# The machine estimate by which the scheduler fills the queues is exchanged

## The chip, the cores and the metric

The kernel runs on one core of a Trainium2 chip. The metric is the device time of one execution in microseconds. Five engines work beside each other, each from a queue of its own that it takes in order: TensorE (PE; its weight loads are listed as PEld), VectorE (DVE), ScalarE (ACT), GpSimd (POOL) and SyncE (SP). All DMAs of this kernel are issued from SP's queue (SPq).

## The reference

One layer over 512 positions of width 1024: two branches of the normed input, a causal depthwise convolution and a recurrent scan, are gated, merged and projected, and a feed-forward block with a squared relu follows. What is computed, shortened:

```python
def hybrid_layer(x, c, ...):
    mod = jax.nn.silu(c) @ w_ada + b_ada
    shift1, scale1, gate1, shift2, scale2, gate2 = jnp.split(mod, 6, axis=-1)
    h = modulate(rms_norm(x, g_norm1), shift1, scale1)
    u = h @ w_in
    u_conv, u_rwkv, u_gate = jnp.split(u, [2 * CONV_DIM, 2 * CONV_DIM + RWKV_COLS], axis=-1)
    y_conv = conformer_conv(u_conv, ...)       # 31 taps, layer norm, silu, @ w_pw
    y_rwkv = rwkv7_mix(u_rwkv, ...)            # the scan below, group norm, gate, @ w_o
    g_conv, g_rwkv = jnp.split(jax.nn.sigmoid(u_gate), N_BRANCH, axis=-1)
    merged = g_conv * y_conv + g_rwkv * y_rwkv
    x = x + gate1[:, None, :] * (merged @ w_out)
    h2 = modulate(rms_norm(x, g_norm2), shift2, scale2)
    ff = jnp.square(jax.nn.relu(h2 @ w_ff1)) @ w_ff2
    return x + gate2[:, None, :] * ff

def step(S, inp):                              # rwkv7_scan, once per position and head
    r_t, w_t, k_t, v_t, a_t, b_t = inp
    Sa = jnp.einsum('bhij,bhj->bhi', S, a_t)
    S = S * w_t[:, :, None, :] + Sa[..., None] * b_t[:, :, None, :] + v_t[..., None] * k_t[:, :, None, :]
    y = jnp.einsum('bhij,bhj->bhi', S, r_t)
    return S, y
```

## The kernel before

Activations lie with features on the 128 partitions and the 512 positions along the free axis. Every large product is a *dense block*: `wload` (L211) has SP load a 1024 x 128 piece of weights into `raw` (two buffers), ScalarE casts it to `wH` (L215) and GpSimd forms the rest `wL` (L216); `wmul` (L219) then issues 24 matmuls of 512 columns into one of three PSUM buffers `mm`, eight times the three of L223, L224 and L225. The span has 142 such loads.

The scan is done in four groups `g` of four heads, in eight chunks of 64 positions. For each group the program traces, in this order:

- `group_solve` (L704 to L736): a triangular solve on VectorE, 31 steps of two small operations (L721, L723) between transposes (L714, L729, L731).
- `window`: dense blocks whose products go elsewhere. "c" is a convolution block (two dense blocks, L516 and L520, then 31 taps on VectorE in `weighted_sum`, L145), "g" a gate block. `WINDOWS` says which stand ahead of the chain and which behind it.
- `group_solve2` (L738 to L756): 128 small matmuls (L747, L753).
- `group_chain` (L758 to L807): for each chunk, on TensorE L767 and L769; ScalarE copies the result to `F` (L772); TensorE L776; ScalarE and VectorE copy it to `UV` (L778, L779); TensorE L784; VectorE forms `sp` and the new state `S` (L791, L792, in the first chunk L788). Each of these needs the one before, and the next chunk needs `S`. The outputs `Y` (L799, L801) hang on it.
- `group_k` and `group_prep` of the next group: its k, r and v blocks, each followed by `shifted` (ScalarE L263, VectorE L264), the decays, BK, AR, transposes (L653, L675) and the products pG (L663); then `group_post` of this one.

After the fourth group come the norm of the convolution, the products with w_pw, w_o and w_out, and the feed-forward blocks.

The order on each queue is made in three ways. Up to L477 (about the first 70 us) `tc.manual_schedule()` keeps the written order. Everything behind it is ordered by the scheduler of the TileContext: as it closes, it plays the program through an estimate of the machine and, whenever an engine can take something, appends to that engine's queue the ready instruction with the best priority. The priority is the place in the program, shifted by `forward(...)` with the numbers of `FORWARD` (one per section and group). Third, `tc.issue_after`, `after_dense` and `amid` pin single pieces behind a given matmul of their own engine. An engine then takes its queue strictly as it stands: what is queued behind an instruction that waits, waits too.

```python
FORWARD = {
    "k": (10, 10, 10, 10), "solve": (127, 153, 48, -153), "window": (0, 7, -47, -43), "chain": (-98, 348, 51, 37),
    "post": (64, 3, 0, 359), "between": (49, 49, 49, 49), "norm": (300,), "silu": (-100,), "amid": (500,),
}
```

The estimate is used for the order alone. Which semaphores an instruction waits for follows from the data and from the buffers, and holds whatever the estimate thought. The context is opened in `kernel`:

## Time and profile before

| what | value |
|---|---|
| median of three runs | 1150.29 us (1146.22 to 1151.23) |
| the profiled execution, its time | 1150.57 us |
| its span, first to last instruction | 1148.8 us |
| TensorE busy | 1066.7 us (93%) |
| VectorE busy | 765.2 us (67%) |
| ScalarE busy | 494.8 us (43%) |
| GpSimd busy | 429.5 us (37%) |
| mean granted TensorE clock | 0.969 |

A busy time is the sum of an engine's records in the profiled execution; a share is of the span. The granted clock is a share of full speed; TensorE has two levels, 2.4 GHz (1.00) and 1.2 GHz (0.50), and a mean between them says how long it stood at either. Times inside the trace are counted from the start of the span.

### The profile page before, as it was taken

The numbers are of one execution on the slowest core, as the hardware profiler recorded it, in microseconds if no ns is written. First come the engines' busy times: TensorE is split into PE (matmuls) and PEld (weight loads), VectorE is DVE, ScalarE is ACT, GpSimd is POOL, SyncE is SP. The second block draws the span as 40 slices with busy tenths as digits, with TensorE's granted clock in tenths as the row PEclk, the third lists the DMA queues.
The fourth block names the chain that finished last, engine by engine and source line by source line (L and its number), as shares of the span: only waits on it lengthen the run. The fifth ranks groups of instructions, "written<-read, shape, count | busy, mean of one in ns | idle before, by whom it ended". The sixth has DMA issues, their size and how long they took to land.

```text
span 1148.8 us, 16008 instructions
## 1 busy us (share of the span) xinstructions
PE 1066.7 (93%) x6290; PEld 818.6 (71%) x6290; DVE 765.2 (67%) x1145; ACT 494.8 (43%) x805; POOL 429.5 (37%) x237
## 2 busy tenths in 40 slices
PE   6898999998799989999979999998999999999997
PEld 5675776666566767667656777886888888888886
DVE  5878787789877898688845649788613612522545
ACT  5555534646155473365566412334413322422331
POOL 4744242243222334125431234453444444444441
PEclk9999799998899999999978999999999999999998
DMA  9622142112321125112636779952333333333332
GB/s 321 217 71 69 47 138 75 51 52 73 99 91 51 42 69 175 48 47 65 202 106 195 232 243 335 284 158 67 92 95 107 93 92 94 107 93 92 98 101 76
DMA packets 188922, 136.73 MB, mean 119 GB/s; under 512 B 5424, under 2 KB 162480, under 8 KB 188848
## 3 DMA queue, kind: packets, MB, share of 16 engines
q1 hardware_dynamic: 188848, 135.73, 38.4%
q8 instruction: 49, 0.80, 0.3%
q14 instruction: 25, 0.20, 0.1%
HBM read 121.55 MB, written 14.16 MB: 118 GB/s over the span
## 4 chain that ended last, share of the span: by engine, by line
PE 65%; DVE 19%; ACT 6%; DMA 5%; issue 3%; POOL 2%; SPq 0%; DVEq 0%; ACTq 0%; POOLq 0%
PE mm L223 16%; PE mm L224 16%; PE mm L225 16%; DVE acc L145 4%; PE pG L663 2%; ACT wH L215 1%; PE Y L801 1%; DMA adaw<-in_w_ada_dram 1%; PE Y L799 1%; PE ch L767 1%; PE ch L776 1%; DVE t2k L251 1%; PE ch L784 1%; DVE t2k L1022 1%; POOL wL L216 1%
## 5 line engine op out<-in xcount | busy, mean ns | idle before, releaser
L216 POOL TENSOR_TENSOR wL<-raw,wH 128x1024 fp32r<-128x1024 f32 x142 | 341.7, 2406 | 592.9 <-ACT wH L215 503.6
L223 PE MATMUL mm<-b,wH 128*128 128x512 f32 x720 | 292.0, 406 | 4.1 <-ACT cv L516 2.9
L225 PE MATMUL mm<-b,wL 128*128 128x512 f32 x720 | 291.0, 404 | 3.7 <-POOL wL L216 2.9
L224 PE MATMUL mm<-b,wH 128*128 128x512 f32 x720 | 291.2, 404 | 2.2 <-DVE b L1032 2.1
L215 ACT CAST wH<-raw 128x1024 fp32r<-128x1024 f32 x142 | 149.1, 1050 | 290.7 <-PE mm L224 238.9
L145 DVE SCALAR_TENSOR_TENSOR acc<-z,vt,acc 128x512 f32<-128x512 f32 x232 | 173.1, 746 | 1.8
L223 PEld LDWEIGHTS mm<-b,wH 128*128 128x128 f32 x720 | 136.9, 190 | 36.4 <-issue 3.5
L225 PEld LDWEIGHTS mm<-b,wL 128*128 128x128 f32 x720 | 137.0, 190 | 36.0 <-POOL wL L216 3.7
L224 PEld LDWEIGHTS mm<-b,wH 128*128 128x128 f32 x720 | 137.0, 190 | 33.5 <-DVE b L1032 3.5
L224 PE MATMUL mm<-g,wH 128*128 128x512 f32 x328 | 128.2, 391 | 1.2 <-DVE g L1024 0.9
L223 PE MATMUL mm<-g,wH 128*128 128x512 f32 x328 | 128.4, 391 | 0.0
L225 PE MATMUL mm<-g,wL 128*128 128x512 f32 x328 | 127.8, 390 | 0.0
L1022 DVE TENSOR_TENSOR t2k<-t2k 128x512 f32<-128x512 f32 x32 | 73.1, 2288 | 57.7 <-ACT t2k L1019 57.4
L1066 DVE SCALAR_TENSOR_TENSOR x<-mm,cols,x 128x512 f32<-128x512 f32 x31 | 23.3, 751 | 114.3 <-PE mm L225 114.3
L224 PEld LDWEIGHTS mm<-g,wH 128*128 128x128 f32 x328 | 61.6, 188 | 15.4 <-DVE g L1024 2.2
L223 PEld LDWEIGHTS mm<-g,wH 128*128 128x128 f32 x328 | 61.6, 188 | 14.0 <-ACT g L1023 1.2
L225 PEld LDWEIGHTS mm<-g,wL 128*128 128x128 f32 x328 | 61.6, 188 | 12.7 <-issue 0.2
L1023 ACT CAST g<-t2k 128x512 fp32r<-128x512 f32 x32 | 19.8, 621 | 72.7 <-DVE t2k L1022 72.7
L663 PEld LDWEIGHTS pG<-AR,BK 64*128 64x128 f32 x256 | 27.2, 204 | 14.2 <-DVE G L666 4.9
L663 PE MATMUL pG<-AR,BK 64*128 64x128 f32 x256 | 32.3, 306 | 5.1 <-DVE G L666 2.0
L1024 DVE TENSOR_TENSOR g<-t2k,g 128x512 fp32r<-128x512 f32 x32 | 23.4, 736 | 19.9 <-ACT g L1023 19.9
L723 DVE TENSOR_TENSOR Y<-tm,Y 128x126 f32<-128x126 f32 (+22 forms) x124 | 31.8, 257 | 3.4
(292 smaller groups left out, 1538.8 us busy)
## 6 DMA issues: line engine op xcount, KB each, us to landing
raw<-in_w_ff_dram SPq DMA_DIRECT2D x64, 512.0 KB, 4.1
raw<-in_w_in_dram SPq DMA_DIRECT2D x54, 512.0 KB, 3.7
adaw<-in_w_ada_dram SPq DMA_DIRECT2D x10, 1024.0 KB, 7.0
t2k<-gate SPq DMA_DIRECT2D x24, 256.0 KB, 3.8
adac<-in_w_ada_dram SPq DMA_DIRECT2D x24, 256.0 KB, 3.4
wa<-in_w_ada_dram SPq DMA_DIRECT2D x11, 512.0 KB, 5.3
gate<-cv SPq DMA_DIRECT2D x16, 256.0 KB, 2.2
raw<-in_w_pw_dram SPq DMA_DIRECT2D x8, 512.0 KB, 4.2
```

The lines of the kernel that those rows point to most:

```text
L145: dve.scalar_tensor_tensor(dst if i == n - 1 else so_far, row, col, so_far, ALU.mult, ALU.add)
L215: act.copy(wH, raw)
L216: last_low[0] = pool.tensor_tensor(wL, raw, wH, ALU.subtract)
L223: steps.append(pe.matmul(acc, wH[:, kc, :], aH(kc), start=kc == 0, stop=False))
L224: steps.append(pe.matmul(acc, wH[:, kc, :], aL(kc), start=False, stop=False))
L225: steps.append(pe.matmul(acc, wL[:, kc, :], aH(kc), start=False, stop=kc == KC - 1))
L663: pe.matmul(pgs[e][:, i, :], BK[64 * e:64 * e + 64, c, C * e:C * e + 2 * C], G.AR[64 * e:64 * e + 64, b, c, :], start=True, stop=True)
L723: dve.tensor_tensor(X[:, s + 1:32, 0:w], tv, X[:, s + 1:32, 0:w], ALU.add)
L1022: dve.tensor_tensor(t, t, t, ALU.mult)
L1023: act.copy(rH(f), t)
L1024: dve.tensor_tensor(rL(f), t, rH(f), ALU.subtract)
L1066: dve.scalar_tensor_tensor(x1(j), acc, ada[:, 40 + j:41 + j], x1(j), ALU.mult, ALU.add)
```

## The change

One argument is added where the TileContext is opened: the scheduler plays the program through its timeline simulation, another estimate of the same machine, and fills the queues by the times that this gives. The program that is traced is the same, with its priorities, pins, buffers and sizes.

```diff
-    with tile.TileContext(nc) as tc:
+    with tile.TileContext(nc, schedule_with_timeline_sim=True) as tc:
         tile_block(tc, *args)
```

## Rows read from the trace of the kernel before

**Rows 1.** The page's part 1, TensorE: busy us, share of the span, instructions.
```profile
PE 1066.7 (93%) x6290; PEld 818.6 (71%) x6290; DVE 765.2 (67%) x1145; ACT 494.8 (43%) x805; POOL 429.5 (37%) x237
```

**Rows 2.** Busy time by stretch: us, busy (x instructions) per engine, clock, DMA share, GB/s.
```profile
0.00:70.00 70.00, 55.59 (x273) 43.15 (x274) 50.56 (x58) 36.38 (x59) 42.58 (x38) 0.95 0.70 221
70.00:170.00 100.00, 92.38 (x430) 71.56 (x429) 80.08 (x145) 54.68 (x88) 37.70 (x28) 0.93 0.30 88
170.00:225.00 55.00, 53.96 (x555) 35.77 (x554) 42.45 (x67) 31.44 (x63) 11.49 (x9) 1.00 0.22 68
225.00:320.00 95.00, 78.52 (x397) 59.21 (x393) 83.69 (x163) 38.34 (x65) 32.67 (x20) 0.91 0.26 79
320.00:375.00 55.00, 52.23 (x542) 34.42 (x542) 43.35 (x68) 30.22 (x62) 11.22 (x8) 1.00 0.20 61
375.00:453.00 78.00, 71.90 (x385) 55.07 (x385) 69.02 (x132) 37.39 (x64) 29.05 (x16) 1.00 0.30 91
453.00:506.00 53.00, 53.00 (x547) 34.93 (x546) 40.40 (x67) 29.96 (x61) 12.07 (x7) 1.00 0.20 62
506.00:595.00 89.00, 77.95 (x445) 55.81 (x445) 67.81 (x136) 51.13 (x83) 39.48 (x24) 0.95 0.37 118
595.00:650.00 55.00, 49.47 (x523) 33.75 (x523) 32.27 (x57) 31.21 (x65) 9.48 (x4) 0.86 0.60 192
650.00:800.00 150.00, 142.52 (x663) 115.15 (x663) 112.72 (x137) 49.46 (x65) 60.29 (x25) 1.00 0.71 224
800.00:1120.00 320.00, 318.88 (x1409) 262.27 (x1408) 127.26 (x100) 99.87 (x128) 138.73 (x58) 1.00 0.33 95
1120.00:1149.00 29.00, 20.33 (x142) 17.48 (x140) 15.55 (x26) 4.67 (x9) 4.77 (x2) 0.84 0.22 75
```

**Rows 3.** Order of time in the first chain: start us, us, engine, line, operation, tiles.
```profile
183.56 0.26 ACT L772 COPY F<-ch 128x128 f32<-128x128 f32 x1
...
184.63 0.45 PE L776 MATMUL ch<-F,G 64*64 64x64 f32 x8
...
185.42 0.28 DVE L779 COPY UV<-ch 64x128 f32<-64x128 f32 x1 [1.05 <-ACT UV L778]
...
186.82 0.45 PE L784 MATMUL ch<-UV,bkT 128*64 128x64 f32 x8
...
188.19 0.29 DVE L792 TENSOR_TENSOR S<-sp,PC 128x128 f32<-128x128 f32 x1
...
189.13 0.34 PE L767 MATMUL ch<-S,AR 64*64 64x64 f32 x4
```

**Rows 4.** Who waited for whom, TensorE, whole span: us, times, longest.
```profile
PE pv L675 <- DVE t2k L264: 8.1, 1, 8.1
...
PE mm L225 <- POOL wL L216: 2.9, 2, 1.7
```

**Rows 5.** The same view, TensorE, 595 to 650.
```profile
PE sW L747 <- DVE s L729: 6.4, 1, 6.4
```

**Rows 6.** Order of time, 279 to 298: the last dense matmul, and the shift.
```profile
279.39 0.39 PE L225 MATMUL mm<-b,wL 128*128 128x512 f32 x1
...
297.20 0.74 DVE L264 SCALAR_TENSOR_TENSOR t2k<-mm,vt,t2k 128x511 f32<-128x511 f32 x1
```

**Rows 7.** Groups of instructions, VectorE: busy us, mean ns, idle before.
```profile
L792 DVE TENSOR_TENSOR S<-sp,PC 128x128 f32<-128x128 f32 x24 | 15.0, 624 | 0.1
```

**Rows 8.** Order of time at 208, GpSimd and VectorE.
```profile
208.29 2.38 POOL L216 TENSOR_TENSOR wL<-raw,wH 128x1024 fp32r<-128x1024 f32 x1 [10.71 <-ACT wH L215]
...
208.85 1.98 DVE L792 TENSOR_TENSOR S<-sp,PC 128x128 f32<-128x128 f32 x1
```

**Rows 9.** Who waited for whom, SP's queue, whole span.
```profile
SPq L213 <- POOL wL L216: 696.1, 130, 23.3
```

**Rows 10.** Order of time, TensorE, at 604 in the last chain.
```profile
604.13 0.69 PE L776 MATMUL ch<-F,G 64*64 64x64 f32 x8 [1.88 <-ACT G L734]
...
605.58 0.70 PE L784 MATMUL ch<-UV,bkT 128*64 128x64 f32 x8
```

## The prediction

> **What bounds the kernel now.** I read the page's busy shares first: TensorE works in 1066.7 us of the 1148.8 us span [rows 1]. A change that removes no instruction can therefore win only from the 82 us in which TensorE stands idle, and from the time it spends at the lower of its two clock levels. The second view is the busy time in twelve stretches, cut where the stages of the kernel change [rows 2]. Here the reader is to see three kinds of stretch. The first 70 us (idle 14.4) are written out by hand in manual_schedule and the estimate cannot move them. From 800 on the program is a plain row of dense blocks, each with 24 matmuls that wait for nothing but their weights: idle 1.1 of 320 us, then 8.7 in the tail, where each step needs the one before. So only 70 to 800 can change. In it lie four chain stages (170, 320, 453, 595), idle 1.0, 2.8, 0.0 and 5.5, together 9.3 us; four stages between them (70, 225, 375, 506), idle 7.6, 16.5, 6.1 and 11.1, together 41.3 us; and the outputs (650 to 800), idle 7.5. The sum, 58 us, is all that order alone can give back, with the clock beside it.
>
> The third view is the order of time inside a chain [rows 3]. A step of the chain is a TensorE product, a copy on ScalarE or VectorE, and the next product. F is copied by 183.82 (183.56 + 0.26) and its product L776 starts at 184.63; UV is done at 185.70 and L784 starts at 186.82; S is done at 188.48 and L767 starts at 189.13. Each product is queued 0.81, 1.12 and 0.65 us behind its operand, mean 0.86, with dense matmuls in front of it. That is a margin: the default estimate holds the copies for slower than they are, and puts three or four dense matmuls (0.226 us each, 318.88 us for 1409 in rows 2) where the chip needs about one fewer each time. The margin costs nothing, because those matmuls must run somewhere.
>
> The fourth view is who waited for whom. The two longest single waits of TensorE in the movable part are 8.1 us for the shift of v (L264) [rows 4] and 6.4 us for the solve's transpose L729 [rows 5]. In the first, a last dense matmul starts at 279.39 and L264 only at 297.20 [rows 6]: VectorE's queue holds solve steps and conv taps ahead of it. This looks like a wrong idea in the default estimate of what is ready when, and a better one could take it away.
>
> **The change, part by part.** No instruction is added or removed, and no size changes. What changes is the clock by which the scheduler decides which ready instruction goes next into each queue. The priorities (FORWARD), the issue_after edges and the numbers of buffers stand. Five queues are refilled: TensorE, VectorE, ScalarE, GpSimd and SP.
>
> Chain steps. There are 32 F copies, 32 UV copies and 28 S updates, 92 steps with a margin. A new estimate that prices the copies lower queues the product closer to its operand. What the chip then adds (a copy that stands behind a longer instruction on its engine, an S step that is slowed) is no longer covered. Ends: nothing (margin kept; a shorter chain can return at most the 9.3 us its stages idle now), and all of it, 92 x 0.86 = 79 us. I take one dense matmul too few in half the steps: 92 x 0.5 x 0.226 = 10.4 us. The nearest row is the last chain, which has its filler in short supply already and idles 5.5 us; three more like it instead of 3.8 us would add 12.7 us, which is about the same.
>
> S steps beside GpSimd. L792 lasts 0.28 us mostly, but its mean is 0.624 us over 24 [rows 3, 7]: the excess is 24 x (0.624 - 0.284) = 8.2 us. The long one at 208.85 (1.98 us) lies inside the wL conversion that GpSimd began at 208.29 [rows 8]. At 1.7 us each the excess is about five of 24. GpSimd is busy 0.21 of the first chain stage [rows 2], and 0.21 x 24 = 5: the present order has as many collisions as chance would give. The new order draws them again: 0, with ends of -8.2 (none) and +33 (all 24; 24 x 1.7 - 8.2). I add 1.7 us: one more such step, met without its margin.
>
> The Trainium skill, "SBUF — State Buffer", section "Who interferes with whom", says that a VectorE instruction with two SBUF inputs and a GpSimd instruction that reads SBUF lock each other out, and that issue order decides who waits; L792 has such inputs only through sp and PC, and its end at 210.83, just behind the conversion's at 210.67, agrees. By that rule alone, an order that starts every conversion just ahead of an S step would cost the +33 us end; one that keeps them apart the -8.2.
>
> Stages between the chains. The same program (k, the preparation, solve, post) stands there four times with different windows, in four different orders: 7.6, 16.5, 6.1, 11.1 us, mean 10.3 [rows 2]. I take these as four draws of what an order gives: a new draw has the same mean, so 0. Ends: all four like the best, 4 x 6.1 - 41.3 = -16.9 us (most of it the 8.1 us wait of rows 4); all like the worst, 4 x 16.5 - 41.3 = +24.7 us. What is late next when a wait goes is VectorE: it is busy 83.7 of 95 us in the worst of these stages [rows 2].
>
> The clock. It is granted at 0.91 from 225 to 320 and 0.86 in the last chain, 1.00 in the other chains [rows 2]. At 2.4 and 1.2 GHz a mean of 0.86 is 28% of 55 us, 15.4 us, at the lower level, in which 7.7 us of work is lost. These two stages hold the two longest waits [rows 4 to 6]. If a chain idles more, it falls there too: I take half of one such stage, +3.9 us, with ends of -4.3 (half of the 8.6 us of the 0.91 stage regained) and +23 (three more chains like the last).
>
> Loads. SP's queue is refilled too: weight loads, gate, conv and vb stores and reloads pass each other. SP waits 696 us in all for wL to free a raw buffer, and TensorE waits only 2.9 us for wL [rows 4, 9]: loads are early, and the two raw buffers, not SP's order, set when they start. Nothing; if a small load gets ahead wrongly, one block of 24 x 0.226 = 5.4 us. The outputs (650 to 800): 0, within 7.5 us either way.
>
> Sum: 1150.57 us for the profiled execution (span 1148.8 and 1.8 around it, 0.3 us above the median of 1150.29) + 10.4 + 1.7 + 0 + 3.9 = 1166.6 us.
>
> **The rivals.** *Faster, about 1129.* The mechanism is the VectorE queue between the chains: an estimate that ends a dense block when the chip does puts L264 and the z products behind their block instead of behind the taps, and lets the solve's transposes end before TensorE has emptied its row. It takes the -16.9 us of the best draw and the -4.3 us of clock: 1129.4. For it speaks that the order in [rows 6] leaves TensorE standing for work that was ready; against it that VectorE is busy 88% of that stage [rows 2], so that putting L264 first makes the solve later. It decides if the chains keep at least a third of their margin.
>
> *Much slower, about 1206.* The timeline lets a queue take in whatever is ready, ahead of the engine. Then a whole dense block (5.4 us) stands in front of each of the first products of a chain, the dense work of the stage is used up in some five steps, and the remaining 18 of 23 run bare. A bare step is seen at 604.13 to 605.58, 1.45 us [rows 10], of which the products themselves take 0.45 at full clock [rows 3]: 1.0 us idle at most, 0.9 taken. Per chain 18 x 0.9 - 2.3 = 13.9, four times 55.6: 1206. Against it: priorities put the chain first, if they are still asked when the engine comes free.
>
> *No change, 1150.6.* The two estimates agree closely enough, or the issue_after edges and priorities decide nearly everything, so that the order is the old one where it matters. Against it: 92 steps with margins that come from the estimate itself.
>
> **How the numbers follow.** The forecast, a moderate loss (1157 to 1190), has 0.43; much slower 0.16; no change 0.13; faster 0.28. Half a per cent, 5.8 us, is about what a measurement of this kernel can tell from no change. So faster 0.28, same 0.13, slower 0.59. The range reaches from the full faster case, 1128, to just past the much slower one, 1208; about one in ten lies beyond on either side. The forecast's own range is 1157 to 1190.
>
> **What would show it.** In the trace after, a right forecast has products L767, L776 and L784 starting within 0.4 us of their operands, TensorE's waits on F, UV and S above what they are now, chain stages idle by 4 us or more each, and a granted clock below 1.00 in two or more of them; the stages before 70 and after 800 as long as now. The faster rival shows chains as full as now and no wait of several us on L264 or L729. The much slower one shows chain stages of over 65 us with runs of 24 dense matmuls between two products. It would be wrong altogether if the time moved before 70 or after 800, or if ScalarE, GpSimd or a load became what TensorE waits for most.

## The result, and the profile after

| | before | after |
|---|---|---|
| median of four runs | 1149.33 us (1146.22 to 1151.23) | 1258.4 us (1257.93 to 1259.71) |
| span of the profiled execution | 1148.8 us | 1256.5 us |
| TensorE busy | 1066.7 us | 1092.8 us |
| mean granted TensorE clock | 0.969 | 0.887 |

The ratio is 1.0954 (1.0927 to 1.0981): the kernel lost 109 us where 16 were forecast, and the time lies outside the range. Part 1 of the page after, against [rows 1]:

```profile
PE 1092.8 (87%) x6290; PEld 865.3 (69%) x6290; DVE 768.5 (61%) x1145; ACT 486.8 (39%) x799; POOL 430.3 (34%) x237
```

The same 6290 matmuls are 26.1 us longer, because more of them ran at the lower clock. TensorE's idle time went from 82.1 to 163.7 us (1256.5 - 1092.8): 81.6 more. The two make the 107.7 us by which the span grew.

Where the idle time lies is read from busy time by stretch, cut by the kernel's own marks: a chain stage goes from the first `sW` product (L747) to its last copy `Yt` (L802). [Rows 2] was cut at times of the kernel before; for a like comparison here is before again with the marks as cuts, first its four chain stages, then what follows each (columns: us; busy and instructions of PE, PEld, DVE, ACT, POOL; granted clock; DMA share; GB/s).

```profile
173.20:232.30 59.10, 58.13 (x595) 38.73 (x596) 45.77 (x76) 30.89 (x65) 12.22 (x9) 1.00 0.21 63
321.60:380.10 58.50, 57.32 (x594) 38.17 (x595) 45.00 (x73) 32.05 (x66) 12.35 (x9) 1.00 0.18 56
453.40:514.10 60.70, 59.20 (x601) 39.27 (x600) 47.49 (x76) 31.21 (x65) 14.44 (x8) 1.00 0.20 61
597.20:651.10 53.90, 50.53 (x538) 34.64 (x539) 30.61 (x56) 29.31 (x64) 7.28 (x4) 0.87 0.62 198
...
232.30:321.60 89.30, 71.60 (x335) 54.56 (x335) 78.81 (x154) 37.20 (x61) 30.52 (x19) 0.90 0.27 81
380.10:453.40 73.30, 67.20 (x332) 51.36 (x332) 66.17 (x127) 35.97 (x60) 27.93 (x16) 1.00 0.31 96
514.10:597.20 83.10, 71.40 (x391) 51.48 (x393) 62.52 (x127) 51.42 (x79) 39.31 (x23) 0.94 0.37 122
651.10:800.00 148.90, 141.42 (x648) 114.19 (x649) 112.18 (x136) 49.41 (x65) 60.29 (x25) 1.00 0.71 224
```

And the same stages of after:

```profile
203.30:270.50 67.20, 49.39 (x517) 36.85 (x516) 61.16 (x99) 27.62 (x61) 7.69 (x8) 0.61 0.11 34
358.30:422.60 64.30, 50.28 (x539) 38.31 (x538) 54.70 (x91) 26.62 (x58) 10.11 (x8) 0.68 0.13 40
513.30:578.00 64.70, 49.27 (x530) 37.28 (x529) 53.96 (x90) 26.73 (x59) 8.76 (x6) 0.64 0.11 34
671.10:765.70 94.60, 84.62 (x696) 65.55 (x696) 41.19 (x69) 29.84 (x63) 19.09 (x8) 0.91 0.61 195
...
270.50:358.30 87.80, 80.96 (x380) 63.87 (x381) 69.84 (x133) 39.41 (x66) 32.08 (x18) 0.93 0.29 90
422.60:513.30 90.70, 84.71 (x413) 68.02 (x415) 50.85 (x109) 40.70 (x67) 31.94 (x17) 0.94 0.31 95
578.00:671.10 93.10, 60.33 (x330) 43.00 (x330) 51.23 (x110) 47.42 (x78) 32.79 (x20) 0.76 0.30 95
765.70:915.00 149.30, 125.26 (x530) 98.81 (x531) 110.94 (x128) 50.21 (x69) 52.32 (x22) 0.90 0.54 171
```

Length less TensorE's busy time gives the idle time. The four chain stages idled 1.0, 1.2, 1.5 and 3.4 us; now they idle 17.8, 14.0, 15.4 and 10.0: 50.2 us more. The three stages between them change by -10.9, -0.1 and +21.1 us. The 150 us behind the last chain lose 16.6. All the rest (the first 203 us, and what follows 915) accounts for +4.8. In the first three chains the clock fell from 1.00 to 0.61, 0.68 and 0.64.

The length of a chain hides part of the loss. The first three took 178.3 us before and take 196.2 now, only 17.9 more. But the groups of TensorE's instructions, taken over the same stretches, count 331 dense matmuls (L223, L224, L225) in them before, and 110 after. The 221 others run elsewhere, at 0.226 us each [rows 2]: by this estimate 50 us of span that the chains used to cover for nothing. Counted by their starts, 430, 266 and 299 dense matmuls run now in the stages ahead of these three chains (70 to 203, and the two between), where 294, 212 and 218 ran before; the stage ahead of the first is 30 us longer, where 136 more at 0.226 us would make 31. The last chain is another case: it holds 228 now, 86 before, and grew from 53.9 to 94.6 us, with 142 fewer behind it. The rows of L223, a third of the dense matmuls (the count is behind the x): the stage ahead of the first chain, before and after, then the first chain, before and after.

```profile
L223 PE MATMUL mm<-b,wH 128*128 128x512 f32 x98 | 39.7, 405 | 0.0
L223 PE MATMUL mm<-b,wH 128*128 128x512 f32 x143 | 56.5, 395 | 1.1 <-DVE t2k L264 1.1
...
L223 PE MATMUL mm<-b,wH 128*128 128x512 f32 x37 | 16.2, 437 | 0.0
L223 PE MATMUL mm<-b,wH 128*128 128x512 f32 x8 | 3.6, 445 | 0.0
```

What a chain looks like now, against [rows 3] (TensorE, then ScalarE, then VectorE; start us, us, what it does; in brackets the idle time before it and who ended it):

```profile
259.47 0.49 PE L767 MATMUL ch<-S,AR 64*64 64x64 f32 x4 [0.57 <-DVE S L792]
...
261.16 0.69 PE L776 MATMUL ch<-F,G 64*64 64x64 f32 x8
262.21 0.48 PE L801 MATMUL Y<-UV,G 128*64 128x64 f32 x2 [0.36 <-ACT UV L778]
262.60 0.70 PE L784 MATMUL ch<-UV,bkT 128*64 128x64 f32 x8
263.09 0.42 PE L801 MATMUL Y<-UV,G 128*64 128x64 f32 x2
265.69 0.48 PE L767 MATMUL ch<-S,AR 64*64 64x64 f32 x4 [2.18 <-DVE S L792]
...
260.70 0.27 ACT L772 COPY F<-ch 128x128 f32<-128x128 f32 x1 [0.74 <-PE ch L769]
...
259.24 3.12 DVE L145 SCALAR_TENSOR_TENSOR acc<-z,vt,acc 128x512 f32<-128x512 f32 x4
262.27 0.28 DVE L779 COPY UV<-ch 64x128 f32<-64x128 f32 x1
```

F is ready at 260.97 and its product starts at 261.16; UV at 262.55 and 262.60. Between two products stand only the outputs `Y`, no dense matmul. The margin that the prediction read in three steps, 0.86 us in the mean, is gone here, and the engine waits for S for 2.18 us instead. Of all 88 products in the chains that need a copy or a state just made, 9 start within 0.25 us of it before, and 64 after. Four conv taps stand in a row in VectorE's queue between the chain's own steps. The stretch around it, as busy time, has TensorE at its lower level throughout:

```profile
250.00:275.00 25.00, 14.55 (x150) 11.40 (x146) 24.41 (x40) 7.11 (x19) 4.29 (x5) 0.50 0.03 12
```

Who waited for whom, TensorE and then all engines, whole span:

```profile
PE mm L223 <- DVE t2k L264: 19.5, 5, 6.3
PE Y L801 <- ACT UV L778: 18.3, 24, 5.2
PE ch L767 <- DVE S L792: 17.3, 17, 2.2
PE sW L747 <- DVE s L729: 11.7, 1, 11.7
...
DVE G L666 <- PE pG L663: 78.8, 18, 11.4
```

The wait of pv for L264 [rows 4] is gone, as the faster rival wanted, but dense matmuls now wait for L264 for 19.5 us, and the longest wait for L729 grew from 6.4 [rows 5] to 11.7. The last line is new in kind: VectorE stands still for 78.8 us because the products pG (L663), which open the next group's solve, come late from TensorE. Before, that row of the groups read 5.3 us:

```profile
L666 DVE TENSOR_TENSOR G<-pG,ct 128x512 f32<-128x512 f32 x32 | 21.5, 682 | 5.4 <-PE pG L663 5.3
```

### The profile page after: what moved, and what is told of

The parts are those of the page before. It is cut to its first block, busy times and chain, and to the rows that moved or that the text cites. A ratio compares the mean times of both kernels' runs of the same rounds, so it can differ in the third digit from the quotient of the medians.

```text
span 1256.5 us, 16024 instructions
## 1 busy us (share of the span) xinstructions
PE 1092.8 (87%) x6290; PEld 865.3 (69%) x6290; DVE 768.5 (61%) x1145; ACT 486.8 (39%) x799; POOL 430.3 (34%) x237
## 4 chain that ended last, share of the span: by engine, by line
PE 57%; DVE 9%; ACT 5%; issue 4%; DMA 3%; POOL 1%; SPq 0%; DVEq 0%; ACTq 0%; POOLq 0%
PE mm L223 16%; PE mm L225 16%; PE mm L224 16%; DVE acc L145 3%; PE pG L663 2%; PE g L834 1%; ACT wH L215 1%; DMA t2k<-yo 1%; PE Y L801 1%; PE prn L183 1%; DMA raw<-in_w_out_dram 1%; DMA raw<-in_w_o_dram 1%; DVE t2k L980 0%; DVE Yt L815 0%; PE mm L1080 0%
## 5 line engine op out<-in xcount | busy, mean ns | idle before, releaser
L223 PE MATMUL mm<-b,wH 128*128 128x512 f32 x720 | 291.1, 405 | 26.0 <-DVE t2k L264 19.5
L224 PE MATMUL mm<-b,wH 128*128 128x512 f32 x720 | 288.9, 401 | 4.4 <-DVE b L1032 4.4
L225 PE MATMUL mm<-b,wL 128*128 128x512 f32 x720 | 288.6, 401 | 2.0 <-POOL wL L216 2.0
L215 ACT CAST wH<-raw 128x1024 fp32r<-128x1024 f32 x142 | 149.1, 1050 | 314.4 <-PE mm L224 255.4
L223 PEld LDWEIGHTS mm<-b,wH 128*128 128x128 f32 x720 | 139.2, 193 | 58.6 <-DVE t2k L264 20.9
L224 PEld LDWEIGHTS mm<-b,wH 128*128 128x128 f32 x720 | 139.0, 193 | 34.9 <-DVE b L1032 4.8
L225 PEld LDWEIGHTS mm<-b,wL 128*128 128x128 f32 x720 | 138.5, 192 | 34.1 <-POOL wL L216 3.6
L223 PE MATMUL mm<-g,wH 128*128 128x512 f32 x328 | 128.5, 392 | 3.7 <-ACT wH L215 3.7
L224 PE MATMUL mm<-g,wH 128*128 128x512 f32 x328 | 127.1, 389 | 0.0
L225 PE MATMUL mm<-g,wL 128*128 128x512 f32 x328 | 126.5, 390 | 0.0
L1022 DVE TENSOR_TENSOR t2k<-t2k 128x512 f32<-128x512 f32 x32 | 75.7, 2370 | 60.5 <-ACT t2k L1019 57.8
L1066 DVE SCALAR_TENSOR_TENSOR x<-mm,cols,x 128x512 f32<-128x512 f32 x31 | 23.3, 750 | 114.8 <-PE mm L225 114.8
L223 PEld LDWEIGHTS mm<-g,wH 128*128 128x128 f32 x328 | 61.6, 188 | 18.7 <-ACT wH L215 5.8
L225 PEld LDWEIGHTS mm<-g,wL 128*128 128x128 f32 x328 | 61.6, 188 | 13.1 <-issue 0.2
L224 PEld LDWEIGHTS mm<-g,wH 128*128 128x128 f32 x328 | 61.6, 188 | 12.7
L666 DVE TENSOR_TENSOR G<-pG,ct 128x512 f32<-128x512 f32 x32 | 21.1, 687 | 78.8 <-PE pG L663 78.8
L801 PE MATMUL Y<-UV,G 128*64 128x64 f32 x256 | 38.5, 283 | 18.3 <-ACT UV L778 18.3
L801 PEld LDWEIGHTS Y<-UV,G 128*64 128x64 f32 x256 | 30.5, 186 | 25.0 <-ACT UV L778 22.9
L767 PE MATMUL ch<-S,AR 64*64 64x64 f32 x224 | 22.5, 288 | 17.8 <-DVE S L792 17.3
```

The costliest lines, as they stand in the source:

```text
L215: act.copy(wH, raw)
L223: steps.append(pe.matmul(acc, wH[:, kc, :], aH(kc), start=kc == 0, stop=False))
L224: steps.append(pe.matmul(acc, wH[:, kc, :], aL(kc), start=False, stop=False))
L225: steps.append(pe.matmul(acc, wL[:, kc, :], aH(kc), start=False, stop=kc == KC - 1))
L666: dve.tensor_tensor(G.G[:, b, e, cq * 4:cq * 4 + 4, :], pgs[e], gmask.unsqueeze(1).to_broadcast([P, 4, P]), ALU.mult)
L767: pe.matmul(pf[ot:ot + 64, b, :], G.AR[lo:lo + 64, b, c, 0:C], S[lo:lo + 64, b, :], start=True, stop=False)
```

## The theories

The order of TensorE's queue can be read off the two programs as they are built. Call a step of the chain *bare* when no dense matmul stands between its product and the small product of chain or solve before it (outputs `Y` in between don't count). Of the chains' 88 products that need the step before them (32 times L776, 28 times L784, 28 times L767; the prediction counted 92 by the copies) 2 are bare before and 71 after: 20 of 22 in each of the first three chains, 11 of 22 in the last. Where a step isn't bare, before has 1 to 13 dense matmuls in front of it, and after 8 to 34. In each of the first three chains of after, the first four products are bare already, then one block of 24 stands in front of two products, and the rest is bare: their dense work had run ahead of the chain, as the counts above show. Only the last chain has dense matmuls (12 to 34) in front of its early products.

The timeline's description of the machine holds a number for each engine: how many instructions its queue may take in ahead of the engine. It is 35 for TensorE and 12 for VectorE, ScalarE and GpSimd. *Theory A:* by that number TensorE's queue, as the scheduler plays it, swallows dense blocks as soon as they are ready, ahead of chain products and pG that become ready a little later; what has been taken in can't be passed any more, whatever its priority. Then the dense work is spent before the chain needs it. Against it stood that another queue's order does the harm, that the priorities or the estimate's prices do, and, once the first runs were in, different accounts of what A leaves over.

## Experiments on which queue carries the loss

Two kernels fill one queue in the order of the one estimate and the others by the other. The order is taken from a first tracing of the same program, and held by dependencies on the same engine, which need no semaphore:

```diff
+    order = _order_of(False)          # every queue's order under the default estimate
     with tile.TileContext(nc, schedule_with_timeline_sim=True) as tc:
         tile_block(tc, *args)
+        _queue_as(tc, order, ['PE'])  # each instruction of this queue behind the one before it
```

**TensorE as before, the rest by the timeline.**

> TensorE's queue is held in the order of the kernel before (behind the hand-written first 70 us); VectorE, ScalarE, GpSimd and SP are filled by the timeline simulation around it. Theory A, the loss of 109 us lies in TensorE's order (dense blocks taken in ahead of the chain's products): 1150 to 1175 us, chains with 2 to 10 dense matmuls before each product. Theory B, it lies in the other queues (conv taps and solve on VectorE, casts, loads): above 1225 us.

Measured: 1210.31 us (1208.13 to 1212.5), ratio 1.0521 (1.0493 to 1.0549). Less than half of the loss went away, and neither theory's number held. TensorE's own waits show where it stands:

```profile
PE bkt L653 <- DVE BK L629: 22.6, 4, 8.5
PE sX L753 <- ACT s L750: 14.5, 5, 9.8
PE Y L799 <- ACT Sd L806: 7.9, 7, 2.9
```

These waits are for VectorE and ScalarE, whose queues the timeline filled around this order of TensorE. TensorE's queue has the 2 bare steps of before again, and the time is still 61 us longer, so bare steps alone don't make the time, and this experiment bounds nothing from below. What holding a queue costs by itself was not measured: no run holds all queues in one estimate's order.

**TensorE as after, the rest by the default estimate** (`_order_of(True)`, context without the argument).

> The mirror of the run before: TensorE's queue is held in the order of the changed kernel, the other four are filled by the default estimate around it. Theory A: 1235 to 1270 us, with chains that stand bare and a granted clock near 0.5 there. Theory B: below 1180 us.

Measured: 1247.06 us (1245.73 to 1248.39), ratio 1.084 (1.0818 to 1.0863). The new order of TensorE alone brings 98 of the 109 us, as A expected. With the run above (61 us) the parts sum to more than the whole: they are not additive, and only the direction can be read from such mixtures.

**The chain's priority raised.** All four chains are shifted far ahead of everything else in the program:

```diff
-... "chain": (-98, 348, 51, 37),
+... "chain": (2000, 2000, 2000, 2000),
```

> The changed kernel with the chain's priority raised far above all other work (FORWARD chain 2000 in every group). Theory C: the chain gets in front of the dense blocks and most of the loss returns, below 1200 us. Theory A: priority is asked only when an instruction is taken in, so the dense block is there already: 1245 to 1270 us, order nearly the same.

Measured: 1258.09 us in one run, the time of after; the queue of TensorE is nearly the same too. Theory C's time, below 1200 us, is excluded. The run agrees with A's account, that the dense block is already in the queue when a chain product becomes ready, and that priority is asked only when an instruction is taken in.

## Experiments on how far the queue is filled ahead

These change the one number and nothing else in the program:

```diff
+    from concourse.hw_specs import TRN2Spec
+    TRN2Spec.ENG_ISSUE_QUEUE_DEPTH[mybir.EngineType.PE] = 2      # the library has 35
     with tile.TileContext(nc, schedule_with_timeline_sim=True) as tc:
```

> The changed kernel with one number of the timeline's description of the machine altered while it schedules: how many instructions TensorE's queue may take in ahead of the engine, 2 in place of 35. Theory A with this cause: dense matmuls in front of a chain product fall from 15 to 24 to about 4 to 12 and lie in all chunks; two thirds of the loss or more return, 1150 to 1185 us. Theory C, the timeline prices copies and products otherwise and the priorities settle the rest: no change, 1245 to 1265 us.

> The changed kernel with 8 instructions taken in on TensorE, between 2 (1166 us) and 35 (1258 us). Theory A: a dose, 1175 to 1225 us, about 7 to 11 dense matmuls before each product while there are any, chains bare in their last two or three chunks. If 35 is only one side of a threshold: 1166 or 1258 us within 8 us.

> The changed kernel, with the timeline letting TensorE take in 16 instructions ahead instead of 35. Theory A (the time follows how far TensorE is filled ahead, through the steps of the chain left bare): between 1183 (at 8) and 1258 (at 35); its first three chains have some 14 of 23 steps bare against about 20 at 35 and some 6 at 8, which by proportion gives 1183 + 75 x 8/14 = 1226; taken 1205 to 1245. A rival (only the full 35 overruns, as a step): within 10 us of 1183.

> The changed kernel, with the timeline letting VectorE, ScalarE and GpSimd take in 2 instructions ahead instead of 12, TensorE unchanged at 35. Theory A (TensorE's taking-in is the cause): 1245 to 1270, as the changed kernel, since its TensorE queue again has no dense matmul in front of nearly all steps of the first three chains. Theory F (a good part is the overrun of the other engines): 1230 to 1245, by the 16.7 us that are left with TensorE alone at 2.

| taken in ahead | bare steps of 88 | by chain | time, us | ratio (interval) |
|---|---|---|---|---|
| default estimate (before) | 2 | 0, 0, 0, 2 | 1149.3 | |
| TensorE 2 | 14 | 1, 11, 0, 2 | 1166.18 | 1.0146 (1.0123 to 1.0169) |
| TensorE 8 | 27 | 9, 11, 6, 1 | 1182.6 | 1.0285 (1.0229 to 1.034) |
| TensorE 16 | 43 | 14, 15, 13, 1 | 1202.3 | 1.0463 (1.0425 to 1.0501) |
| TensorE 35 (after) | 71 | 20, 20, 20, 11 | 1258.4 | 1.0954 (1.0927 to 1.0981) |
| TensorE 35, the other three 2 | 69 | 20, 20, 20, 9 | 1262.03 | 1.0983 (1.0939 to 1.1027) |

With 2 in place of 35, 92 of the 109 us return; 8 and 16 lie in between in order; the other engines' number alone returns nothing. For 16, A's interval (1205 to 1245) was just missed on the low side; its proportion was too steep. So theory A is shown for the main part, the share of the loss that TensorE's number alone gives and takes.

Against the kernel before as measured beside it, each additional bare step goes with 1.39, 1.28, 1.34 and 1.58 us (16.7/12, 32.1/25, 54.9/41, 109.1/69). That is a rate along this one knob, and no law for other kernels: 2 bare steps gave 1210 us above, and 71 gave 1247 where the other queues were old. The knob also changes when pG comes. Part 1 and VectorE's row for pG move with it, for 2, 8 and 16 in turn:

```profile
PE 1063.8 (92%) x6290; PEld 826.5 (71%) x6290; DVE 773.4 (67%) x1145; ACT 488.1 (42%) x800; POOL 431.7 (37%) x237
...
L666 DVE TENSOR_TENSOR G<-pG,ct 128x512 f32<-128x512 f32 x32 | 21.3, 685 | 18.7 <-PE pG L663 18.6
```

```profile
PE 1070.0 (91%) x6290; PEld 837.5 (71%) x6290; DVE 773.2 (66%) x1145; ACT 486.0 (41%) x799; POOL 430.0 (36%) x237
...
L666 DVE TENSOR_TENSOR G<-pG,ct 128x512 f32<-128x512 f32 x32 | 21.2, 680 | 23.4 <-PE pG L663 23.3
```

```profile
PE 1077.0 (90%) x6290; PEld 848.4 (71%) x6290; DVE 773.1 (64%) x1145; ACT 486.5 (41%) x799; POOL 429.5 (36%) x237
...
L666 DVE TENSOR_TENSOR G<-pG,ct 128x512 f32<-128x512 f32 x32 | 21.3, 683 | 44.8 <-PE pG L663 44.7
```

VectorE's wait for pG reads 18.6, 23.3, 44.7 and (after) 78.8 us; TensorE's busy time for the same matmuls 1063.8, 1070.0, 1077.0 and 1092.8. Both the late pG and the lost clock move with the same number.

## Experiments on what is left at 2

At 2 the kernel is still 16.7 us slower than before, and old TensorE among new queues 61 us. Four runs asked whether VectorE's order is to blame, or the number of the other engines: the first two for the 61 us, the last two for the 16.7. Each holds one or two queues in the order of before, or sets more numbers to 2, or both:

```diff
+    for e in ("PE", "DVE", "Activation", "Pool"):
+        TRN2Spec.ENG_ISSUE_QUEUE_DEPTH[getattr(mybir.EngineType, e)] = 2
...
+        _queue_as(tc, order, ['PE', 'DVE'])
```

**TensorE as before, all four numbers 2** (`['PE']` with the loop).

> TensorE in the order of the kernel before, the other four queues filled by the timeline, which may take in 2 instructions ahead on VectorE, ScalarE and GpSimd in place of 12. The 61 us that the other queues cost beside the old TensorE order: theory D, they come from the same taking in, on those engines: 1150 to 1180 us. Theory E, they come from where the timeline puts conv taps and preparation on VectorE when the TensorE order does not fit: 1195 to 1220 us, no change.

Measured: 1200.93 us (1198.87 to 1202.98), ratio 1.0444 (1.0385 to 1.0504): little less than the 1210.31 without the numbers. That is in theory E's interval, not in D's.

**TensorE and VectorE as before, no number changed.**

> TensorE and VectorE in the order of the kernel before; ScalarE, GpSimd and SP filled by the unchanged timeline around them. Theory E: the 61 us vanish, 1148 to 1168 us. Theory D: part of them stays with ScalarE and GpSimd, above 1180 us.

Measured: 1197.86 us (1195.82 to 1199.9), ratio 1.0417 (1.0358 to 1.0477). Theory E fails here: with TensorE's and VectorE's orders both those of before, 47 us remain, and they come with the orders of the other three queues. The waits of TensorE here (`sW` for the solve is 8.4 us over the whole span before, 6.4 of it in [rows 5]):

```profile
PE sW L747 <- DVE s L729: 15.2, 3, 10.2
PE pv L675 <- DVE t2k L264: 9.5, 1, 9.5
```

**TensorE's number 2, VectorE as before** (`['DVE']`).

> The run with 2 instructions taken in on TensorE, and VectorE held in the order of the kernel before. The 16.7 us that are left there: theory E, they are VectorE's order: 1142 to 1158 us. Otherwise (TensorE's own new order, loads) 1162 us or more.

Measured: 1189.72 us (1186.23 to 1195.91), ratio 1.0337 (1.0291 to 1.0382): 23 us worse than with VectorE left to the timeline. Theory E failed with the wrong sign; the other bound, 1162 us or more, held. All four mixtures with an old queue among new ones cost 39 to 61 us, so the method can't split a rest of 17 us.

**All four numbers 2, every queue by the timeline** (the loop alone).

> The changed kernel, with the timeline letting VectorE, ScalarE and GpSimd take in 2 instructions ahead instead of 12, and TensorE 2 instead of 35. Theory A (what is lost comes from TensorE's taking-in; the 16.7 us that are left with TensorE alone at 2 come from how well the four queues fit together, not from the other three's depth): within 10 us of 1166, so 1156 to 1176. Theory F (the 16.7 us are the same overrun on VectorE, whose taps then stand four in a row ahead of the chain's own steps): 1140 to 1155. In its TensorE queue the second group keeps eight bare steps at its end, which the kernel before has not; each bare step idles about 0.9 us, so some 7 us are expected to remain under either theory.

Measured: 1164.34 us (1163.03 to 1168.21), ratio 1.0144 (1.011 to 1.0178). As A expected, the other engines' number adds nothing that can be told from 1166.18. The queue has 9 bare steps here (0, 7, 0 and 2), 5 fewer than with TensorE's number alone, and it is no faster by the 7 us that the rate above would give: that rate can't be carried over.

Where the rest lies can be read, if not why. The chain stages of the kernel with TensorE's number 2:

```profile
176.60:242.30 65.70, 65.27 (x635) 45.88 (x634) 54.34 (x90) 33.02 (x68) 18.02 (x11) 1.00 0.21 62
321.40:386.50 65.10, 55.38 (x578) 40.16 (x578) 57.99 (x92) 29.22 (x61) 11.99 (x9) 0.85 0.17 50
453.40:520.80 67.40, 67.22 (x643) 47.07 (x643) 55.57 (x90) 32.02 (x66) 17.13 (x10) 1.00 0.23 68
593.00:664.30 71.30, 59.20 (x591) 41.87 (x592) 43.00 (x74) 35.62 (x72) 13.59 (x6) 0.90 0.69 220
```

The first and the third are as full as before, at clock 1.00. The second idles 9.7 us: it is the one whose last steps are bare, 11 of them. The fourth idles 12.1; its first L776 waits for G, the result of the second solve:

```profile
PE ch L776 <- ACT G L756: 6.2, 1, 6.2
```

Together the chains idle 22.4 us against 7.0 before; these 15.4 are nearly all of the 16.3 us by which the idle time of the whole differs (98.4 against 82.1).

**TensorE's number 1.** If fewer were always better, the rest should vanish here.

> The changed kernel, with the timeline letting TensorE take in 1 instruction ahead instead of 35 (2 gave 1166.2, 8 gave 1182.6, 16 gave 1202.3). In the TensorE queue that this gives, nearly every step of the chains has one or two dense matmuls in front of it, none runs bare in a row, and the last chain holds some 46 dense steps' matmuls where take-in 2 holds three times as many. Theory G (the 16.7 us that are left at 2 lie in the last chain, which takes 71.3 us there against 53.9 in the kernel before because it holds 41 dense steps of three matmuls against 29: 36 matmuls more at 0.43 us are 15.6): the last chain takes at most 55 us and the whole 1140 to 1160. Rival H (one or two dense matmuls, 0.4 to 0.9 us, are too few to cover what VectorE and ScalarE need between two products, so each step leaves TensorE idle and the clock falls): 1175 to 1215, with the four chains longer and idle of TensorE over 110 us.

Measured: 1449.08 us (1446.57 to 1455.95), ratio 1.2622 (1.2567 to 1.2676). Both theories missed by far. Only 10 of the 88 steps are bare, so the count that ordered the other kernels fails. The order of time in the first chain (TensorE, ScalarE, VectorE) shows another overrun:

```profile
247.93 0.40 PE L224 MATMUL mm<-b,wH 128*128 128x512 f32 x1
261.46 0.69 PE L776 MATMUL ch<-F,G 64*64 64x64 f32 x8 [13.13 <-ACT F L772]
...
257.59 0.78 ACT L143 ACTIVATE acc<-z,vt 128x512 f32<-128x512 f32 x1 [18.98 <-DVE co L145]
...
261.14 0.26 ACT L772 COPY F<-ch 128x128 f32<-128x128 f32 x1
...
243.29 13.42 DVE L145 SCALAR_TENSOR_TENSOR acc<-z,vt,acc 128x512 f32<-128x512 f32 x17
```

TensorE waits 13.13 us for the copy F. F stands in ScalarE's queue behind L143, the start of the next convolution, which waits 18.98 us for a row of taps on VectorE, 17 of them shown. This is one example, not the whole: TensorE idles 287.9 us in this run, and only 78 of them lie in the four chain stages. Its two longest waits in sum are 43.8 us for the cast wH (L215) and 43.1 for UV (L779). How much of the loss is H's, too few dense matmuls in front of a step, is not separated. Whether the numbers of ScalarE and VectorE (12) are its cause was not tried; the order, with the chain's copy behind work that waits for VectorE, is what the trace shows.

No kernel here beat the one before. Open remain the cause of the last 15 to 17 us at 2, and of the order at 1.

## Why the prediction was wrong

**The sign and the place were right, the size was not.** Slower by over half a per cent had 0.59. The first 70 us idle 14.2 us (14.4 before), the 320 us of dense blocks are busy for 318.0 (318.9 before, [rows 2]), no load became a bound, and the loss sits in the chains and around them, as the first part of the prediction said.

**The step that failed is "Chain steps".** It took the new estimate for a new price list: copies priced lower, "one dense matmul too few in half the steps: 92 x 0.5 x 0.226 = 10.4 us". What moved the products was, for 92 of the 109 us, not a price but what the queue takes in. The term was small for its own account too: the margin of 0.86 us that it had read is nearly four dense matmuls of 0.226 us, and it gave up one in half the steps. Margins did vanish (products start 0.05 to 0.19 us after their operands, the sign that the prediction had named for its forecast), but in whole chains. The chains idle 50.2 us more. The end of that term, 79 us, held it; the value taken was a fifth of it.

**The right mechanism stood among the rivals, at 0.16.** "Much slower" let a queue take in whatever is ready, ahead of the engine. Its picture, a dense block in front of each of the first products and the other 18 of each chain bare, holds in the last chain alone, and there 11 are bare. In the first three most of the dense work was spent before the chain began, and the first four steps are bare too. That its 72 bare steps meet the queue's 71, and its 55.6 us of idle time in the chains the measured 50.2, is in part luck: 18 in each chain against 20, 20, 20 and 11; 13.9 us in each against 16.8, 12.8, 13.9 and 6.6. "Against it: priorities put the chain first, if they are still asked when the engine comes free" was the sentence that stood against it; the run with the raised priority gives no sign that they are asked again. That condition could not be read from the trace, so it deserved more than the weight of a mishap. The sign named for it, chain stages of over 65 us, was met only by the first and the last (67.2 and 94.6; 64.3 and 64.7 for the others), since a bare chain lasts about as long as a covered one.

**The rival itself was too small**, and with it the range's end of 1208. Three terms were left at zero or counted for the forecast only:

- The clock. The rival's 55.6 counts none; the forecast's sum has 3.9 us. TensorE's busy time rose by 26.1 us, a little beyond the +23 given as the end, "three more chains like the last". A chain without dense work idles and runs at the lower level in most of its time (0.61 to 0.68 of clock): the two losses come together here and had to be added.
- The stages between the chains: 0, with an end of +24.7. Ahead of the four chains they idle +2.3, -10.9, -0.1 and +21.1 us, +12.4 in sum. The last loses most: VectorE waits 31.4 us there for pG, and the solve ends late for a TensorE that has spent its dense work (it is busy 60.3 of 93.1 us).
- The outputs, "0, within 7.5 us either way": +16.6 us in the 150 us behind the last chain. The longest wait there is 7.5 us of `post` (L829) for VectorE.

The growth of the span, 107.7 us, is made up of what was measured, to the rounding: 50.2 in the chains, these three (26.1, 12.4, 16.6), and 2.5 us in the first 70 us and behind 915. Each of the three had an end on record that points there, but they were treated as independent of the rival.

**S steps beside GpSimd:** 1.7 us were added; L792's mean fell instead from 624 ns [rows 7] to 447:

```profile
L792 DVE TENSOR_TENSOR S<-sp,PC 128x128 f32<-128x128 f32 x24 | 10.7, 447 | 0.3
```

That is 24 x 0.177 = 4.2 us less, inside the bounds and of no weight. The count behind it is as the prediction estimated: five of the 24 lasted over 1 us before, each while a GpSimd operation ran, and three do after; all others take 0.27 to 0.29 us. **Loads:** TensorE's wait for wL is 2.0 us (2.9 before), as forecast. **The faster rival** got a part of what it asked for: pv's wait for L264 is gone, and the stage between the first two chains idles 10.9 us less, a tenth of the loss elsewhere. But other matmuls wait 19.5 us for L264 instead, and L729 is later.

## What to carry to other kernels

Before exchanging the estimate by which queues are filled, ask at which moment it picks an instruction: when the engine is free, or when a slot ahead of it is. Where a short dependent chain lives on independent filler, a queue that takes in filler early can spend it before the chain comes; raising the chain's priority did not mend that here. And price a rival with everything it causes: idle time, the clock that falls with it, and the engines that stand behind the starved one.

## What was not expected

A chain stage lasts about as long with 331 dense matmuls in three of them as with 110 (178.3 and 196.2 us): the filler was nearly free, and its price appears only where it is moved to. Eight products L776 took 0.45 us at full clock [rows 3] and 0.69 us here at a granted 0.50, so in a bare chain such products fill a third of a step's mean of 2.07 us (the three steps from 259.47 to 265.69 last 6.22). And fewer taken in is not always better: 2 is 17 us above the kernel before, 1 is 300 us above it.
